# A stage's buffers begin at the weights' address modulo 256, written orders made anew, x loaded first

## The chip, the cores and the metric

The kernel runs on one core of a Trainium2 chip. The metric is the device time of one execution in microseconds (us), the median of several runs. Engines are named as in the profile: PE is TensorE (PEld its weight loads), DVE is VectorE, ACT is ScalarE, POOL is GpSimd, SP is SyncE; an engine's name with a q is its queue, which waits and issues DMAs.

## The reference

A bidirectional encoder of two layers on `x` of 256 tokens by 1024 features, everything in float32. Each layer has three residual parts, so there are six stages:

```
x <- LN(alpha*x + 0.5*SwiGLU_1(x))
x <- LN(alpha*x + Mixer(x))        # layer 0: bidirectional chunkwise mLSTM, layer 1: windowed attention
x <- LN(alpha*x + 0.5*SwiGLU_2(x))
swiglu(x, w_in, w_out) = (silu(x @ w_in[:, :2816]) * (x @ w_in[:, 2816:])) @ w_out
```

The four SwiGLU parts (1024 by 5632 and 2816 by 1024 weights each) are most of the work. The mixers are a projection, a chunk of small per-head work, and an output projection.

## The kernel before

**Float32 products in three passes.** A float32 operand is split into two parts of the type fp32r, a high part (ACT copies and rounds it) and a low part (DVE subtracts the high part from the original). `mm3` (lines 598 to 601) then issues three matmuls: high by high, high by low, low by high. The stationary operand, which a weight load brings into the array before each matmul, is 128 columns of activations. The moving operand, which streams past it, is 512 columns of weights.

**Weights.** `Weights.load` issues a DMA of 512 KB from HBM into a raw buffer of one of two kinds: four `w_raw` tiles that live for the whole kernel, and in the SwiGLU stages eight more, `s_raw`, that belong to the stage. `Weights.split` (lines 382 to 404) lets ACT write one of ten `w_hi` tiles and DVE one of ten `w_lo` tiles from it. The SwiGLU stages compute most of the up projection with seven block products instead of eight (`seven`, line 835; `product`, line 822), for which DVE adds raw weight blocks in place and POOL issues DMAs that add a block from HBM onto a raw buffer.

**Stationary operands.** `xT_hi` and `xT_lo` hold the transposed activations and live for the whole kernel. A stage owns `S1` to `S4` (sums of blocks of the transposed activations, for the seven products), `h` and `hc` (the transposed result of SiLU times up, for the down projection), in the attention stage `q`, `kp` and others, and temporaries `t`.

**Where buffers lie.** Whole-kernel tiles come from ordinary pools. Stage buffers share one region of `4 * WHOLE` bytes per partition at the upper end of SBUF; each stage lays its own buffers out in it from the bottom (`Stage.new`, lines 342 to 353), every buffer size rounded up to 32 bytes, in the order in which the code asks for them. Worked out from the sizes in the code, the start addresses are:

| buffers | start address modulo 256 before |
|---|---|
| `w_raw`, `w_hi`, `w_lo`, `x`, `xT_hi`, `xT_lo`, `neg_id` | 96 |
| `ident` | 128 |
| SwiGLU stages: `h`, `s_raw`, `t`, `S1` to `S4`, `hc` | 64 |
| mLSTM stage: `v` (four tiles) | 64, 96, 128, 160 |
| mLSTM stage: `q`, `k`, gate rows, `wt`, `a`, `ln_g`, `ln_b` | 224 |
| attention stage: `kp`, `sc`, `dist`, `v`, `q` | 224 |
| attention stage: `ln_g`, `ln_b`, `pr0`, `pr1`, `o` | 96 |

**The order of the work.** Code that calls an engine only records the call (`Engine`, line 304). `Program.issue` (line 292) then issues all calls in the order written down in `ORDER` (steps between call numbers), and `Rooms.take` gives each request the buffer that the lists in `SLOTS` name. So the order on every engine's queue and the choice of each buffer in a ring are written lists, made beforehand by a planner that is not part of the kernel. All issued calls carry line 301 in the profile; operations are told apart by the tiles that they write and read.

**The start.** `load_x` (line 558) loads `x` in four parts of 128 tokens by 512 features on ACT's queue. PE transposes a part, ACT and DVE split the result into `xT`, and the first products follow. PE also runs two lots of ten transposes of `ident` to bridge the time until `x` lands.

Of the kernel before, what the change touches and what calls it, by code (L numbers as in the profile page):

```python
# [37 lines left out]
WHOLE = 21800  # L38
ORDER = (
# [210 lines left out]
    "mv": ("010101010101"),  # L250
    "rs": ("010101010101"),
    "raw.1": ("30230230230123012301230123012301"),
    "wt.1": ("0123"),
    "a_hir.1": ("0101"),
    "a_lor.1": ("1010"),
    "den.1": ("0101"),
# [77 lines left out]
class Stage:  # L334
# [7 lines left out]
    def new(self, name, n, bufs, dt):  # L342
        tag = name
# [1100 lines left out]
```

## Time and profile before

| | |
|---|---|
| median of 3 runs | 942.94 us (942.77 to 944.59) |
| the profiled execution's own time | 939.63 us |
| its span, first to last instruction | 937.9 us |
| PE busy | 921.9 us (98% of the span) |
| DVE busy | 814.0 us (87%) |
| ACT busy | 578.4 us (62%) |
| POOL busy | 142.3 us (15%) |
| granted TensorE clock | 0.998 |

A row of instruction groups shows the line, the engine, the operation, what it writes and reads, the shapes and the count; behind the first bar the busy time of the group and the mean duration of one in ns; behind the second the engine's idle time just before, and what ended it. A row of the timeline shows start and duration in us. Matmuls overlap: the next starts before the previous has ended, so the step from start to start is what counts, and it is shorter than the duration shown.

### The profile page before, as it was taken

The numbers are of one execution on the slowest core, as the hardware profiler recorded it, in microseconds if no ns is written. First come the engines' busy times: TensorE is split into PE (matmuls) and PEld (weight loads), VectorE is DVE, ScalarE is ACT, GpSimd is POOL, SyncE is SP. The second block draws the span as 40 slices with busy tenths as digits, with TensorE's granted clock in tenths as the row PEclk, the third lists the DMA queues.
The fourth block names the chain that finished last, engine by engine and source line by source line (L and its number), as shares of the span: only waits on it lengthen the run. The fifth ranks groups of instructions, "written<-read, shape, count | busy, mean of one in ns | idle before, by whom it ended". The sixth has DMA issues, their size and how long they took to land.

```text
span 937.9 us, 12265 instructions
## 1 busy us (share of the span) xinstructions
PE 921.9 (98%) x4368; PEld 757.3 (81%) x4368; DVE 814.0 (87%) x955; ACT 578.4 (62%) x813; POOL 142.3 (15%) x202
## 2 busy tenths in 40 slices
PE   8999999999999999999999999999999999999996
PEld 7887888889988888888888888888887688878885
DVE  6998888886798999889899978898978899987985
ACT  6765577556654667566548575665578567665560
POOL 0411201100100111111011102111444211211110
PEclk9999999999999999999999999999999999999999
DMA  9999898557346699889967997885740487998841
GB/s 345 285 284 275 237 284 211 192 180 226 135 174 254 175 276 233 260 247 244 313 212 200 270 281 183 268 240 181 256 132 4 154 250 228 248 292 230 264 126 45
DMA packets 100637, 208.50 MB, mean 222 GB/s; under 512 B 6848, under 2 KB 21200, under 8 KB 100576
## 3 DMA queue, kind: packets, MB, share of 16 engines
q1 hardware_dynamic: 82368, 173.04, 52.3%
q0 software_dynamic: 17632, 33.64, 21.4%
q10 hardware_dynamic: 576, 1.05, 0.3%
q8 instruction: 34, 0.56, 0.2%
q14 instruction: 27, 0.22, 0.1%
HBM read 206.65 MB, written 1.05 MB: 221 GB/s over the span
## 4 chain that ended last, share of the span: by engine, by line
PE 93%; DMA 2%; DVE 2%; ACT 2%; POOL 0%; issue 0%; POOLq 0%; ACTq 0%
PE p L301 93%; DMA x<-in_x_dram 1%; DMA s_raw<-in_ffn_w_in_dram 1%; DVE pr_lor L301 0%; ACT w_hi L301 0%; ACT sc L301 0%; DVE rm L301 0%; DVE x L301 0%; DVE o L301 0%; POOL sc L301 0%; DVE nm L301 0%; ACT q_hir L301 0%; ACT o L301 0%; DVE w_lo L301 0%; POOL sm L301 0%
## 5 line engine op out<-in xcount | busy, mean ns | idle before, releaser
L301 ACT CAST w_hi<-s_raw 128x1024 fp32r<-128x1024 f32 x237 | 242.4, 1049 | 116.4 <-PE p L301 68.0
L301 DVE TENSOR_TENSOR w_lo<-s_raw,w_hi 128x1024 fp32r<-128x1024 f32 x237 | 282.6, 1218 | 25.3 <-ACT w_hi L301 24.3
L301 ACT CAST w_hi<-w_raw 128x1024 fp32r<-128x1024 f32 (+1 forms) x168 | 174.3, 1046 | 85.2 <-PE p L301 43.3
L301 DVE TENSOR_TENSOR w_lo<-w_raw,w_hi 128x1024 fp32r<-128x1024 f32 (+1 forms) x168 | 202.4, 1218 | 27.6 <-ACT w_hi L301 27.3
L301 PE MATMUL p<-w_hi,xT_hi 128*128 128x512 f32 x512 | 203.7, 398 | 0.0
L301 PE MATMUL p<-w_hi,xT_lo 128*128 128x512 f32 x512 | 200.1, 391 | 0.0
L301 PE MATMUL p<-w_lo,xT_hi 128*128 128x512 f32 x512 | 199.7, 390 | 0.3 <-DVE w_lo L301 0.3
L301 PE MATMUL p<-w_hi,h_hir 128*128 128x512 f32 x320 | 127.3, 398 | 0.0
L301 PE MATMUL p<-w_lo,h_hir 128*128 128x512 f32 x320 | 126.4, 395 | 0.0
L301 PE MATMUL p<-w_hi,h_lor 128*128 128x512 f32 x320 | 126.2, 395 | 0.0
L301 PEld LDWEIGHTS p<-w_hi,xT_lo 128*128 128x128 f32 x512 | 96.1, 188 | 20.4
L301 PEld LDWEIGHTS p<-w_lo,xT_hi 128*128 128x128 f32 x512 | 96.4, 188 | 19.3 <-DVE w_lo L301 0.7
L301 PEld LDWEIGHTS p<-w_hi,xT_hi 128*128 128x128 f32 x512 | 96.4, 188 | 18.4
L301 POOL DMA_DIRECT2D s_raw<-in_ffn_w_in_dram x44 | 53.2, 1210 | 341.6 <-DVE s_raw L301 94.2
L301 PE MATMUL p<-w_hi,S_hir 128*128 128x512 f32 x256 | 101.3, 396 | 0.4 <-ACT t L301 0.4
L301 PE MATMUL p<-w_lo,S_hir 128*128 128x512 f32 x256 | 101.2, 395 | 0.0
L301 PE MATMUL p<-w_hi,S_lor 128*128 128x512 f32 x256 | 101.1, 395 | 0.0
L301 PEld LDWEIGHTS p<-w_hi,h_lor 128*128 128x128 f32 x320 | 60.0, 187 | 14.6
L301 PEld LDWEIGHTS p<-w_lo,h_hir 128*128 128x128 f32 x320 | 60.0, 188 | 14.2
L301 PEld LDWEIGHTS p<-w_hi,h_hir 128*128 128x128 f32 x320 | 60.0, 188 | 14.0
L301 PEld LDWEIGHTS p<-w_hi,S_hir 128*128 128x128 f32 x256 | 48.0, 187 | 12.8 <-ACT t L301 1.1
L301 PEld LDWEIGHTS p<-w_lo,S_hir 128*128 128x128 f32 x256 | 48.0, 187 | 12.1 <-DVE w_lo L301 0.4
(201 smaller groups left out, 1195.4 us busy)
## 6 DMA issues: line engine op xcount, KB each, us to landing
s_raw<-in_ffn_w_in_dram SPq DMA_DIRECT2D x104, 512.0 KB, 6.5
w_raw<-in_ffn_w_in_dram SPq DMA_DIRECT2D x56, 512.0 KB, 6.3
s_raw<-in_ffn_w_out_dram SPq DMA_DIRECT2D x55, 512.0 KB, 6.8
s_raw<-in_ffn_w_in_dram POOLq DMA_DIRECT2D x44, 512.0 KB, 6.4
w_raw<-in_ffn_w_out_dram SPq DMA_DIRECT2D x33, 512.0 KB, 6.6
w_raw<-in_ml_w_in_dram SPq DMA_DIRECT2D x24, 512.0 KB, 4.4
w_raw<-in_ffn_w_in_dram POOLq DMA_DIRECT2D x20, 512.0 KB, 7.8
w_raw<-in_at_w_in_dram SPq DMA_DIRECT2D x12, 512.0 KB, 4.2
```

Source lines behind the costliest of these rows:

```text
L301: f(*args, **kw)
```

## The change

Three things change together.

1. `Stage.new` lays out buffers in two directions. Sizes that are multiples of 64 elements (256 bytes) go up from the bottom, the others come down from the end of the region. `WHOLE` falls from 21800 to 21792 elements, so the region begins 32 bytes later: at 96 modulo 256 in place of 64. As a result `h`, `s_raw`, `t`, `S1` to `S4`, `hc`, `q`, `k`, `kp`, `sc`, `dist`, the attention's `v` and all other buffers of whole 256 bytes begin at 96 modulo 256, as the weights do. The small statistics tiles and the mLSTM's `v` tiles (whose rows are 1032 elements long) lie at the end.
2. `ORDER` and most lists of `SLOTS` are written anew. PE's matmuls keep their order, all 4,368 of them; the order on DVE, ACT, POOL and SP differs in many places, and so do the buffers that are taken from the rings.
3. At the start ACT's queue issues all four parts of `x` one behind the other, the first halves of both token blocks ahead of the second halves, and only then loads its table of functions. Before, one part was issued, then the table was loaded, then two parts were issued, and the fourth after ACT's first evacuation. In the new order a copy stands ahead of the recorded table load, so a table load of its own comes ahead of that copy: ACT has one table load more, 7 in place of 6.

```
-WHOLE = 21800
+WHOLE = 21792
 ORDER = (
-    "0 5 35 -34 63 -65 4 1 75 -74 1 109 -108 1 87 -99 13 1 123 -135 13 1 136 21 -156 1 1 1 3 1 -3 4 1 -25 189 "
...
+    "0 1 1 1 2 35 -34 63 -61 1 75 -74 1 89 -88 1 1 1 1 1 1 156 -155 1 1 22 -19 1 -3 4 1 93 -92 13 -18 6 1 -26 27 "
...
 class Stage:
 
     def __init__(self, rooms, bass_, start, key, kinds):
-        self.rooms, self.bass, self.start, self.key, self.top, self.tags = rooms, bass_, start, key, 0, {}
+        self.rooms, self.bass, self.start, self.key, self.top, self.end, self.tags = rooms, bass_, start, key, 0, WHOLE, {}
...
     def new(self, name, n, bufs, dt):
         tag = name
         if tag not in self.tags:
-            self.tags[tag] = self.top, -(-n // 8) * 8
-            self.top += bufs * self.tags[tag][1]
-            assert self.top <= WHOLE, (tag, self.top)
+            size = -(-n // 8) * 8
+            if size % 64 == 0:
+                self.tags[tag] = self.top, size
+                self.top += bufs * size
+            else:
+                self.end -= bufs * size
+                self.tags[tag] = self.end, size
+            assert self.top <= self.end, (tag, self.top, self.end)
         at, step = self.tags[tag]
```

More of the change, by code (lines that the diff above doesn't have):

```diff
@@ L35 @@
 PEND = [6, 4, 6, 6, 6]
-WHOLE = 21800
+WHOLE = 21792
 ORDER = (
[190 rows of a table removed]
[190 rows of a table added]
 )
 SLOTS = {
-    "p": ("0123456702374502145673565365735653567657360521734652017436452071356201735602614735017524360143751237"
-        "4652140704340347043404373470364523145627136050646046506460645465042671503467021354702615340762453127"
-        "046653644534665364354365436127301267503642461641624616461216"),
+    "p": ("0123456702354702147653767367537673765675360721534672015436472051376201537602614537015724360143571235"
+        "4672140504340345043404353450364723147625136070646046706460647467042651703465021374502615760325674310"
+        "562274266746227426476427642310453120754261623263216232623132"),
     "h_hir.0": ("01010"),
@@ L237 @@
     "raw.0": ("012345678192ab034567a2b30514687905182465317908a24b7198025a46183b0256"),
-    "w_hi": ("0123456789012359071346803259714354307568252914307685291430768529143076852940713685472901368547290136"
-        "8547290136854729013685472901368547290681354729806135428137659041628375904162837590416283759041623598"
-        "7041386259704138625970413869725041387692504372519086429375108642937510864293751086429350871642589307"
-        "1642589307164258930716425893071642589713064258197306451302768943751026894375102689437510268943750681"
-        "294308756129"),
+    "w_hi": ("0123456789012359071346891250734154197568252034197685203419768520341976852049731685472093168547209316"
+        "8547209316854720931685472093168547209683154720896315428317650943628175094362817509436281750943621508"
+        "7943186250794318625079431860725943187602594172530986420175398642017539864201753986420159873642570198"
+        "3642570198364257019836425701983642570831964257308196453192867041853926704185392670418539267041859673"
+        "204197856320"),
     "w_lo": ("0123456789012345678901236457890137826945065137829406513782940651378294065172938406795123840679512384"
         "0679512384067951238406795123840679512384067951328406791285304672391850467239185046723918504672398041"
-        "5672813904567281390456728139045672819304567213089546739210854673921085467392108546739205418673049251"
-        "8673049251867304925186730492518673049251867304295186734950281679234508167923450816792345081679235814"
-        "067951238406"),
+        "5672813904567281390456728139045672819304567213089546739210854673921085467392108546739205418673019254"
+        "8673019254867301925486730192548673019254867301295486731950284679231508467923150846792315084679235841"
+        "067954238106"),
     "t.0": ("03242155040312543102435120431"),
@@ L252 @@
     "raw.1": ("30230230230123012301230123012301"),
-    "wt.1": ("0123"),
+    "wt.1": ("3201"),
     "a_hir.1": ("0101"),
-    "a_lor.1": ("1010"),
+    "a_lor.1": ("0101"),
     "den.1": ("0101"),
@@ L261 @@
     "h_lor.2": ("0101010101"),
-    "raw.2": ("a9b78234061ba9578234ab97526830415260b87a32415690b8421650a9b7263850a79b384501a8749b35012694b531802a67"
-        "318a4059216738ba4061783a9b4518203a95"),
-    "t.2": ("1320154023124503241532045132451043524013025410235104253102"),
-    "sc.4": ("4501230145230145230145"),
-    "raw.4": ("20320320320132013201"),
+    "raw.2": ("a564789236041a5789b214a75968b32059634871b92056a3482906531a4796b85317a4b825301872a4b53096a245b0839167"
+        "b081235a9067b841236078b1a4250893b1a5"),
+    "t.2": ("2354210453250143502135401235012403150423451024531240513245"),
+    "sc.4": ("1405231405231405231405"),
+    "raw.4": ("23123123123012301230"),
     "rm.4": ("01201201"),
@@ L270 @@
     "es.4": ("01201201"),
-    "pr0_hir.4": ("01010101"),
+    "pr0_hir.4": ("10101010"),
     "pr0_lor.4": ("01010101"),
@@ L275 @@
     "o.4": ("01010101"),
-    "h_hir.5": ("10101"),
-    "h_lor.5": ("10101"),
-    "raw.5": ("3201320148596732ab0169723b8a04153b849a260b1538749a1b58346792b80a3462"),
-    "t.5": ("02135043125140321450213405214"),
+    "h_hir.5": ("01010"),
+    "h_lor.5": ("01010"),
+    "raw.5": ("1230123058496712ab3069721b8a35041b859a263b0418759a0b48156792b83a1562"),
+    "t.5": ("51024532014035210345102354103"),
 }
```

378 rows, old and new, of the table ORDER are left out of this document.

## Prediction

> **What bounds the kernel now.** I read the page first, then PE's waits, then the groups of instructions, and last the timeline of PE where it runs without a wait.
>
> ```profile
> span 937.9 us, 12265 instructions
> PE 921.9 (98%) x4368; PEld 757.3 (81%) x4368; DVE 814.0 (87%) x955; ACT 578.4 (62%) x813; POOL 142.3 (15%) x202
> ...
> PE 93%; DMA 2%; DVE 2%; ACT 2%; POOL 0%; issue 0%; POOLq 0%; ACTq 0%
> ```
>
> PE is busy for 98% of the span and is 93% of the chain that ended last. What shortens the stream of matmuls shortens the kernel; what happens beside it does not, unless PE comes to wait for it. So the question is how long one matmul takes, and whether its operands' places in SBUF have a part in that.
>
> ```profile
> L301 PE MATMUL p<-w_hi,xT_lo 128*128 128x512 f32 x512 | 200.1, 391 | 0.0
> L301 PE MATMUL p<-w_lo,xT_hi 128*128 128x512 f32 x512 | 199.7, 390 | 0.3 <-DVE w_lo L301 0.3
> L301 PE MATMUL p<-w_lo,h_hir 128*128 128x512 f32 x320 | 126.4, 395 | 0.0
> L301 PE MATMUL p<-w_lo,S_hir 128*128 128x512 f32 x256 | 101.2, 395 | 0.0
> L301 PE MATMUL p<-w_lo,hc_hir 128*128 128x512 f32 x32 | 12.6, 395 | 0.0
> L301 PE MATMUL p<-w_lo,q_hir 128*128 128x512 f32 x32 | 12.6, 393 | 0.0
> L301 PE MATMUL p<-kp_hir,q_lor 128*128 128x512 f32 x16 | 6.3, 395 | 0.0
> ```
>
> All are the same operation: 512 columns of weights past 128 columns of activations. With `xT` as the stationary operand one takes 390 to 391 ns, with `h`, `S` and `hc` 395. `xT` begins at 96 modulo 256, like the moving `w_hi` and `w_lo`; `h`, `S` and `hc` begin at 64. The mean holds starts after transposes too, so I look at stretches without any, by the step from start to start:
>
> ```profile
> 20.11 0.39 PE L301 MATMUL p<-w_lo,xT_hi 128*128 128x512 f32 x1
> 30.99 0.39 PE L301 MATMUL p<-w_lo,xT_hi 128*128 128x512 f32 x1
> ...
> 73.46 0.39 PE L301 MATMUL p<-w_hi,S_hir 128*128 128x512 f32 x1
> 75.80 0.39 PE L301 MATMUL p<-w_lo,S_hir 128*128 128x512 f32 x1
> ...
> 740.84 0.39 PE L301 MATMUL p<-w_lo,q_hir 128*128 128x512 f32 x1
> 744.32 0.40 PE L301 MATMUL p<-w_lo,q_hir 128*128 128x512 f32 x1
> ...
> 920.07 0.39 PE L301 MATMUL p<-w_lo,h_hir 128*128 128x512 f32 x1
> 929.17 0.39 PE L301 MATMUL p<-w_lo,h_hir 128*128 128x512 f32 x1
> ```
>
> `xT`: 48 steps in 10.88 us, 226.7 ns each. `S`: 10 steps in 2.34 us, 234 ns. `q` (at 224): 15 steps in 3.48 us, 232.0 ns. `h`: 39 steps in 9.10 us, 233.3 ns. Three other reasons for the difference can be looked at in the trace. It isn't the form of the code: `product` issues the same twelve matmuls with `xT` and with `S`. Nor is it traffic on SBUF:
>
> ```profile
> core 0: us, PE busy (x) PEld busy (x) DVE busy (x) ACT busy (x) POOL busy (x), PEclk, DMA share, GB/s
> 20.00:31.00 11.00, 11.00 (x51) 9.09 (x50) 11.00 (x11) 7.76 (x10) 1.24 (x2) 1.00 1.04 396
> 920.00:929.00 9.00, 9.00 (x40) 7.21 (x40) 6.96 (x12) 0.59 (x1) 0.56 (x1) 1.00 0.00 0
> 300.00:350.00 50.00, 50.00 (x229) 40.78 (x228) 48.55 (x54) 31.33 (x39) 6.61 (x6) 1.00 0.81 241
> 750.00:800.00 50.00, 50.00 (x228) 40.93 (x228) 49.41 (x57) 34.17 (x43) 6.32 (x5) 1.00 0.81 246
> ```
>
> The fast stretch has the DMA engines and DVE full; the slow one has no DMA and an idle ACT. And it isn't the clock: 1.00 in both. What is left is where the operands lie.
>
> **The change, part by part.**
>
> *Addresses of stationary operands.* `h`, `S` and `hc` go from 64 to 96, the relation that `xT` has now. Their number from the rows: three of a triple, 3 x (320 + 256 + 32) = 1,824. Per matmul the pure stretches give 233.3 - 226.7 = 6.6 ns, in all 12.0 us; the row means give 395 - 390.5 = 4.5 ns, 8.2 us, because around group starts `xT` is slow as well and will stay so. I take the middle, 5.6 ns: 10.2 us. PE's stream has no cover, so this comes off the end. It supposes that being alike modulo 256, or being at 96, is the cause. The `kp` by `q` row speaks against the first form, since both lie at 224 and take 395; but after the change everything is at 96 beside 96, which is the very case of `xT`.
>
> *The attention's operands.* `q`, `kp` go from 224 to 96: 3 x (32 + 16) = 144 matmuls at 232.0 - 226.7 = 5.3 ns, 0.8 us. In that stage short operations of ACT and DVE set part of the time, so between 0 and 0.8; I take 0.5.
>
> *Raw buffers, temporaries, DMA.* `s_raw` moves from 64 to 96, where `w_raw` already lies:
>
> ```profile
> L301 DVE TENSOR_TENSOR w_lo<-s_raw,w_hi 128x1024 fp32r<-128x1024 f32 x237 | 282.6, 1218 | 25.3 <-ACT w_hi L301 24.3
> L301 DVE TENSOR_TENSOR w_lo<-w_raw,w_hi 128x1024 fp32r<-128x1024 f32 x166 | 201.1, 1224 | 26.9 <-ACT w_hi L301 26.6
> L301 ACT CAST w_hi<-s_raw 128x1024 fp32r<-128x1024 f32 x237 | 242.4, 1049 | 116.4 <-PE p L301 68.0 <-DVE s_raw L301 20.7 <-DMA s_raw<-in_ffn_w_in_dram 11.3
> L301 ACT CAST w_hi<-w_raw 128x1024 fp32r<-128x1024 f32 x166 | 173.1, 1051 | 84.4 <-PE p L301 43.3 <-DMA w_raw<-in_ml_w_in_dram 16.3 <-DMA w_raw<-in_at_w_in_dram 5.4
> ...
> s_raw<-in_ffn_w_in_dram SPq DMA_DIRECT2D x104, 512.0 KB, 6.5
> w_raw<-in_ffn_w_in_dram SPq DMA_DIRECT2D x56, 512.0 KB, 6.3
> ```
>
> DVE and ACT take the same within 6 ns, and the landing differs by 0.2 us with ACT's first reason for waiting being PE. So nothing, on either sign.
>
> *`x` first.* PE waits for the parts of `x`:
>
> ```profile
> PE p L301 <- DMA x<-in_x_dram: 2.0, 2, 1.4
> PE p L301 <- DVE w_lo L301: 0.3, 1, 0.3
> ...
> 1.25 1.28 ACT L301 ACT_TABLE_LOAD   x1 [1.25 <-PEq L1431]
> 5.64 0.59 ACT L301 CAST xT_hi<-p 128x512 fp32r<-128x512 f32 x1 [3.10 <-PE p L301]
> 6.63 0.33 ACTq L301 DMA_DIRECT2D x<-in_x_dram  x1
> 7.00 1.14 ACT L301 CAST w_hi<-w_raw 128x512 fp32r<-128x512 f32 x2 [0.78 <-DMA x<-in_x_dram]
> ...
> 6.63 6.12 DMA x<-in_x_dram
> ...
> 11.05 0.39 PE L301 MATMUL p<-w_hi,xT_lo 128*128 128x512 f32 x1
> 12.79 1.09 PE L301 MATMUL p<-ident,x 128*128 128x128 f32 x8 [1.36 <-DMA x<-in_x_dram]
> ```
>
> The fourth part is issued at 6.63, its wait ends 6.12 us later, and PE, done with its step at 11.05 + 0.23, stands until 12.79: 1.5 us. In the new queue four issues (0.33 us for this one) stand ahead of all of ACT's work, so the last goes out within the first 3 us and with the same 6.12 lands by about 9, before PE asks. What it is moved past on ACT's queue are its first evacuation and the table load; on the DMA engines it now competes with SP's first weights, 256 KB at the 396 GB/s of the first window, 0.65 us, for pieces that PE reads after the first twelve matmuls (2.7 us). Late next are ACT's and DVE's halves of `xT`, which PE reads only after twelve more matmuls. The added table load (1.28 us) lies where ACT idles: 3.10 us before 5.64 and 0.78 before 7.00, into which the first copy of weights moves; with that cover gone it costs up to 1.28. So between 0.2 and 1.8 (with the wait for `w_lo`, 0.3, gone too); I take 1.5.
>
> *The written orders.* PE's order stays. With PE faster, DVE has less room: it is busy for 48.55 and 49.41 of 50 us in the two windows above. Each holds some 110 matmuls that get 5.6 ns shorter, 0.6 us, of which DVE's slack covers 1.45 in the one and 0.59 in the other; I take 0.6 us off in all for such places. What the new orders do otherwise can't be seen in this trace: PE is idle for 937.9 - 921.9 = 16.0 us, of which some 8 lie behind its last matmuls (929.17 and one more); the other 8 are start and waits in between, so new orders can hardly win more than 3 us, and I allow the same for a loss; I take 0.
>
> Sum: 10.2 + 0.5 + 1.5 - 0.6 = 11.6 us. Against the profiled execution's own 939.63 us that is 928.0; that execution is 3.3 us below the median, so for the median 942.94 - 11.6 = 931.3 us.
>
> The Trainium skill, in "TensorE: Matmul & The Clock Gate", Part 2, "Step-by-step: what each phase is for", says that PE has two independent SBUF read ports and that loading the next tile's weights doesn't steal read bandwidth from the running matmul. By that rule the addresses would change nothing and the sum would be 1.5 alone. The steps of 226.7 and 233.3 ns don't fit it; no run here yet moves an operand.
>
> **The rivals.**
>
> *The addresses do nothing.* The difference could go with something else that `h`, `S` and `q` share: all lie in the upper part of SBUF, above `xT`. The `kp` by `q` row speaks for it (equal modulo 256, yet 395). Against it: the `h` tiles follow right on `xT`, at a place that is no round number. Then only `x` first is left: 942.94 - 1.5 = 941.4 us. This is the case of the skill's rule too.
>
> *DVE becomes the bound in the SwiGLU stages.* The windows with 97% and 99% speak for it; its 87% over the span and ACT's waiting for PE speak against it. If half of the 10.2 is lost: 936.4 us.
>
> *Slower: results that PE reads next stand behind one more split on DVE.* In the written orders I count 13 results with less than 1.3 us to spare before that now come after one more DVE operation, mostly a `w_lo`. One of them:
>
> ```profile
> 537.32 0.68 DVE L301 TENSOR_TENSOR h_lor<-p,h_hir 128x512 fp32r<-128x512 f32 x1
> ...
> 538.19 0.39 PE L301 MATMUL p<-w_hi,h_lor 128*128 128x512 f32 x1
> ```
>
> Here 0.19 us are spare. Each such place can cost PE up to 1.22 us, all of them 15.9: 947.2 us. It decides from 10 of the 13 on. Against it: many more results come earlier than before, and an order puts a split ahead where DVE would else idle.
>
> **How the numbers follow.** Forecast 0.72, with its own range 927 to 935 (8.2 or 12.0 for the pairs, `x` and orders as above); addresses do nothing 0.10; DVE takes half 0.11; slower 0.07. The range 926.5 to 940 takes in the first and the third. This kernel tells 0.2% (1.9 us) from no change. Faster: 0.72, 0.11 and 0.02 of the second case, 0.85; within: 0.07; slower: 0.07 and 0.01, 0.08.
>
> **What would show it.** The rows of `h`, `S`, `hc` at 390 to 391 ns and a step near 227; `q` and `kp` alike; `xT` unchanged. No wait of PE for `x` after the first, and the eight transposes at about 11.3. DVE and ACT at 1,218 and 1,049 as before. The prediction is wrong if these rows stay at 395, or if PE's waits grow by more than 3 us.

## The result, and the profile after

The changed kernel takes **930.97 us** (median of 4 runs, 928.99 to 933.04) beside 943.77 us for the kernel before in the same comparison: a ratio of **0.9863, 95% interval 0.9835 to 0.9891**. Run once more in a later comparison it stood at 0.9878 (0.9859 to 0.9897), 929.61 beside 942.06 us. That is 11.5 to 12.9 us by the ratios. One execution of the runs below, of the kernel before with less work for DVE, was slow (2369.51 us) and is left out of every figure. The pair of profiled executions shows less, 939.63 against 931.54 us, because the profiled execution of before was the shortest of that kernel that was seen (its times in four comparisons, three medians and a single execution, lie between 941.5 and 943.8).

The page of the changed kernel, its busy times and its chain by engine:

```profile
span 929.8 us, 12210 instructions
PE 912.3 (98%) x4368; PEld 758.3 (82%) x4368; DVE 809.7 (87%) x955; ACT 578.5 (62%) x814; POOL 148.1 (16%) x202
...
PE 78%; DVE 7%; DMA 5%; issue 4%; ACT 4%; POOL 0%; SPq 0%; POOLq 0%; ACTq 0%; DVEq 0%
```

PE's busy time fell by 9.6 us (921.9 to 912.3), and PE is now 78% of the chain that ended last, no longer 93%: DVE, the DMAs and ACT carry the end in more places. Some of its groups of matmuls (busy time, mean ns of one, idle before and what ended it):

```profile
L301 PE MATMUL p<-w_hi,xT_lo 128*128 128x512 f32 x512 | 200.1, 391 | 0.0
L301 PE MATMUL p<-w_lo,xT_hi 128*128 128x512 f32 x512 | 199.7, 390 | 1.1 <-DVE w_lo L301 1.1
L301 PE MATMUL p<-w_lo,h_hir 128*128 128x512 f32 x320 | 124.7, 390 | 0.8 <-DVE w_lo L301 0.8
L301 PE MATMUL p<-w_lo,S_hir 128*128 128x512 f32 x256 | 99.8, 390 | 0.7 <-DVE w_lo L301 0.7
L301 PE MATMUL p<-w_lo,hc_hir 128*128 128x512 f32 x32 | 12.4, 389 | 0.0
L301 PE MATMUL p<-w_lo,q_hir 128*128 128x512 f32 x32 | 12.5, 391 | 0.0
L301 PE MATMUL p<-kp_hir,q_lor 128*128 128x512 f32 x16 | 6.3, 394 | 0.0
```

The first and the last row of a stretch of its PE timeline without a wait, near the end (start, duration):

```profile
912.22 0.39 PE L301 MATMUL p<-w_lo,h_hir 128*128 128x512 f32 x1
921.31 0.39 PE L301 MATMUL p<-w_hi,h_lor 128*128 128x512 f32 x1
```

`h`, `S` and `hc` went from 395 ns to between 389 and 390, `xT` stayed where it was, and the stretch with `h` makes 40 steps in 9.09 us, 227.3 ns each (233.3 before). Over all 1,813 recorded steps to a matmul with `h`, `S` or `hc` as the stationary operand, those above 245 ns left out as waits, the mean went from 233.3 to 227.1 ns: 11.3 us in all. `kp` by `q` hardly moved.

The two windows in which DVE was full before, in the changed kernel:

```profile
300.00:350.00 50.00, 50.00 (x231) 41.30 (x230) 49.61 (x56) 32.00 (x41) 7.70 (x7) 1.00 0.84 249
750.00:800.00 50.00, 50.00 (x232) 41.51 (x231) 48.59 (x54) 33.53 (x42) 7.82 (x7) 1.00 0.86 250
```

Some of PE's waits in it (us in total, times, longest):

```profile
PE p L301 <- DVE w_lo L301: 2.6, 3, 1.1
PE p L301 <- ACT t L301: 1.1, 2, 0.7
PE p L301 <- DMA x<-in_x_dram: 0.7, 1, 0.7
PE p L301 <- DVE pr_lor L301: 0.5, 1, 0.5
```

DVE now fills 99% of the first window, and PE waits 2.6 us for `w_lo` where it was 0.3. The waits for `x` (2.0 before) and for `pr_lo` have shrunk. For the latter, and for one by POOL that will be needed, the rows of the kernel before:

```profile
PE p L301 <- DVE pr_lor L301: 1.6, 2, 1.2
...
PE p L301 <- POOL sc L301: 0.9, 1, 0.9
```

So four things happened at once: shorter steps, new waits for DVE, fewer waits in the attention stage, an earlier `x`. The experiments take them apart.

### The profile page after: what moved, and what is told of

It is laid out like the page before. It is cut to its first block, busy times and chain, and to the rows that moved or that the text cites. A ratio compares the mean times of both kernels' runs of the same rounds, so it can differ in the third digit from the quotient of the medians.

```text
span 929.8 us, 12210 instructions
## 1 busy us (share of the span) xinstructions
PE 912.3 (98%) x4368; PEld 758.3 (82%) x4368; DVE 809.7 (87%) x955; ACT 578.5 (62%) x814; POOL 148.1 (16%) x202
## 4 chain that ended last, share of the span: by engine, by line
PE 78%; DVE 7%; DMA 5%; issue 4%; ACT 4%; POOL 0%; SPq 0%; POOLq 0%; ACTq 0%; DVEq 0%
PE p L301 78%; DVE w_lo L301 4%; DMA s_raw<-in_ffn_w_in_dram 3%; ACT w_hi L301 2%; DMA w_raw<-in_ffn_w_out_dram 1%; DVE s_raw L301 1%; DMA w_raw<-in_ffn_w_in_dram 1%; DVE t L301 0%; ACT wt L301 0%; DMA x<-in_x_dram 0%; SPq L301 0%; DVE x L301 0%; DVE pr_lor L301 0%; ACT t L301 0%; DVE rm L301 0%
## 5 line engine op out<-in xcount | busy, mean ns | idle before, releaser
L301 DVE TENSOR_TENSOR w_lo<-s_raw,w_hi 128x1024 fp32r<-128x1024 f32 x234 | 278.5, 1218 | 28.7 <-ACT w_hi L301 28.5
L301 DVE TENSOR_TENSOR w_lo<-w_raw,w_hi 128x1024 fp32r<-128x1024 f32 (+1 forms) x171 | 205.2, 1215 | 29.2 <-ACT w_hi L301 28.8
L301 ACT CAST w_hi<-w_raw 128x1024 fp32r<-128x1024 f32 (+1 forms) x171 | 176.9, 1046 | 80.4 <-PE p L301 42.9
L301 POOL DMA_DIRECT2D s_raw<-in_ffn_w_in_dram x42 | 51.1, 1218 | 330.1 <-DVE w_raw L301 87.7
```

The source lines that it names most:

```text
L301: f(*args, **kw)
```

## The experiments

Theory A says that the addresses make the gain; theory B gives it to the new written orders. Three runs with one part each, and one with two parts, in one comparison (the kernel before: 941.53 us).

**The addresses alone.** In the kernel before, `WHOLE` only sets where the region begins (229,344 - 4 x `WHOLE`) and a limit, so one number moves it to another place that is 96 modulo 256, with the order and the layout within the region unchanged:

```diff
-WHOLE = 21800
+WHOLE = 21856
```

> The kernel before, its order and its layout, with one number changed: the region of the stages begins 224 bytes lower, at 96 modulo 256 in place of 64, so that h, S and hc lie at 96 like the weights (q and kp come to lie at 0). Theory A, the addresses make the gain: the rows of h, S and hc go from 395 to 390 or 391 ns, the step from start to start from 233.3 to 227.5 ns, and 1,824 matmuls by 5.8 ns give 10.6 us less, a ratio of 0.989. Theory B, the new orders make it: nothing changes, 0.998 to 1.002.

Measured: 933.39 us, ratio 0.9907 (0.9894 to 0.9921), 8.8 us less by the ratio, 8.1 by the medians. Two groups of this run:

```profile
L301 PE MATMUL p<-w_lo,h_hir 128*128 128x512 f32 x320 | 124.5, 389 | 0.0
L301 PE MATMUL p<-w_lo,S_hir 128*128 128x512 f32 x256 | 99.7, 390 | 0.4 <-DVE w_lo L301 0.4
```

Its chain by engine:

```profile
PE 78%; DVE 8%; DMA 7%; ACT 4%; issue 3%; POOL 1%; POOLq 0%; ACTq 0%; SPq 0%; DVEq 0%
```

Theory B falls: with the old orders the rows are at 389 to 390 ns. But about 2.5 us of the 11.3 that the steps give don't reach the end; the chain hands 15% more to other engines. This is taken up below.

**The changed kernel with its region 32 bytes lower.** It keeps the new orders and the early `x` and gives up the alignment:

```diff
-WHOLE = 21792
+WHOLE = 21800
```

> The changed kernel with its region 32 bytes lower, so that h, S, hc, q and kp begin at 64 modulo 256; its orders and its early x stay. Theory A: the rows of h, S and hc are back at 395 ns and the time at that of the kernel before less what the early x gives (1.0 us): a ratio of 0.999, or 0.996 to 1.002 with the orders unknown. Theory B: still 0.987.

Measured: 937.92 us, ratio 0.9962 (0.9949 to 0.9975). The row of `h` is back at 395 ns. So without the addresses the change is still worth 3.6 us, more than the early `x` gives. Its group of `h`:

```profile
L301 PE MATMUL p<-w_lo,h_hir 128*128 128x512 f32 x320 | 126.5, 395 | 0.3 <-DVE w_lo L301 0.3
```

Two of PE's waits in it show where a part of the 3.6 us is:

```profile
PE p L301 <- DVE pr_lor L301: 0.5, 1, 0.5
...
PE p L301 <- POOL sc L301: 0.2, 1, 0.2
```

In the kernel before these two waits, both of the attention stage, were 1.6 and 0.9 us, as shown above. The wait for `w_lo` grew the other way, from 0.3 to 1.4 us.

**`x` first, alone.** In `ORDER` of the kernel before, calls 1 to 3 move up behind call 0:

```diff
-    "0 5 35 -34 63 -65 4 1 75 -74 1 109 -108 1 87 -99 13 1 123 -135 13 1 136 21 -156 1 1 1 3 1 -3 4 1 -25 189 "
+    "0 1 1 1 2 35 -34 63 -65 4 1 75 -74 1 109 -108 1 87 -86 1 123 -122 1 136 21 -156 1 1 1 3 1 -3 4 1 164 -168 5 "
...
```

> The kernel before with one edit: the four loads of x are issued first on their queue. By the prediction 1.5 us less (0.2 to 1.8); by what the changed kernel's first 13 us show, 1.0 us less, because the eight transposes came 1.0 us earlier there: a ratio of 0.999, at the limit of what the runs can tell. The wait of PE for x before those eight goes.

Measured: 940.76 us, ratio 0.9986 (0.9977 to 0.9995): 0.8 us by the medians, 1.3 (0.5 to 2.2) by the ratio. Its profiled execution doesn't show the gain. PE's timeline there:

```profile
5.46 1.12 PE L301 MATMUL p<-ident,x 128*128 128x128 f32 x4 [1.60 <-DMA x<-in_x_dram]
...
10.21 0.63 PE L301 MATMUL p<-w_hi,xT_lo 128*128 128x512 f32 x1
10.64 0.63 PE L301 MATMUL p<-w_hi,xT_hi 128*128 128x512 f32 x1
11.06 0.51 PE L301 MATMUL p<-w_lo,xT_hi 128*128 128x512 f32 x1
11.41 0.40 PE L301 MATMUL p<-w_hi,xT_lo 128*128 128x512 f32 x1
...
13.01 1.03 PE L301 MATMUL p<-ident,x 128*128 128x128 f32 x8
```

The wait before the eight transposes is gone, but they come at 13.01, not at 11.3, for two reasons: the first part of `x` landed 1 us later than in the profile of before (5.46 against 4.49 us; 4.44 in the run below, which has the same edit), and until 11.06 PE ran at half its pace (a step of 0.43 us in place of 0.23). Further on, near 340 and 827 us, PE waits 2.3 us in all for `t`, where it waited 0.4 in the profile of before. Whether the early `x` brings these waits or they are chance, no run shows.

**Both edits in the kernel before**, the region at 96 and `x` first:

```diff
-WHOLE = 21800
+WHOLE = 21856
...
-    "0 5 35 -34 63 -65 4 1 75 -74 1 109 -108 1 87 -99 13 1 123 -135 13 1 136 21 -156 1 1 1 3 1 -3 4 1 -25 189 "
+    "0 1 1 1 2 35 -34 63 -65 4 1 75 -74 1 109 -108 1 87 -86 1 123 -122 1 136 21 -156 1 1 1 3 1 -3 4 1 164 -168 5 "
...
```

> Both edits in the kernel before, its order otherwise kept: the region at 96 and x first. Theory A and x add: 10.6 and 1.0 us, 0.9877, which would be the whole of the change; then the new orders are worth nothing. If the new orders cost what the changed kernel's new stalls suggest (about 3 us more of steps that are too long than before), this one is faster than the changed kernel, 0.984; if they gained, it is slower than the changed kernel's 0.9863.

Measured: 932.78 us, 0.9907 (0.9891 to 0.9922): 0.6 us less than the addresses alone by the medians, nothing by the ratio. Here too the waits for `t` are longer, 1.8 us against 0.7 with the addresses alone, and take a part of the early start back. The changed kernel's 0.9863 and 0.9878 are below it, with intervals that touch, so the new orders gained rather than lost; of the expectation's readings the one that took their new stalls for a loss falls. PE's start in this run:

```profile
8.19 0.75 PE L301 MATMUL p<-w_hi,xT_hi 128*128 128x512 f32 x1
8.77 0.41 PE L301 MATMUL p<-w_lo,xT_hi 128*128 128x512 f32 x1
...
11.33 1.03 PE L301 MATMUL p<-ident,x 128*128 128x128 f32 x8
```

Two of PE's waits in this run, where those of the attention stage are still as in the kernel before:

```profile
PE p L301 <- DVE pr_lor L301: 1.5, 2, 1.2
PE p L301 <- POOL sc L301: 0.9, 1, 0.9
```

In the timeline PE is at full pace from 8.77 us on, as in the profile of before (from 8.75), and the eight transposes come at 11.33 in place of 12.79: 1.46 us earlier.

**Which property of the addresses counts?** A1: the moving operand of the running matmul and the stationary operand of the next must begin alike modulo 256. A2: the place 96 itself. A3 and A4: a distance of 128 or of 64 does too. Four versions of the changed kernel, each with the time of a single execution; the padding of 128 bytes is one line ahead of the weights (in the third ahead of `xT`), the rest is the number. The first is shown; the second has the padding alone, the fourth only the number, 21840.

```diff
-WHOLE = 21792
+WHOLE = 21824
...
+    state.tile([128, 32], F32, name="pad", tag="pad")
     raws = tiles("w_raw", D, F32, RAW_BUFS)
```

> The changed kernel with 128 bytes of padding ahead of the weights and the region moved with them: weights, xT, h, S, hc, q and kp all begin at 224 modulo 256. Theory A1, what counts is that the running matmul's moving operand and the next one's stationary operand begin alike modulo 256: all steps at 227.5 ns, rows of xT, h, S at 389 to 391 ns, time as the changed kernel's, 931 us. Theory A2, what counts is the place 96 itself: every row at 395, xT's too; 5.8 ns for 1,536 + 1,824 matmuls, 19 us more, 950 us. The kp by q row of the kernel before (both at 224, 395 ns) speaks for A2.

> The same padding, the region left at 96: weights and xT at 224; h, S, hc, q and kp at 96. A1: xT stays at 390 to 391 ns, h, S and hc go back to 395: 1,824 by 5.8 ns, 10.6 us more than the changed kernel, 941 us. A2 for the stationary operand alone: the reverse, xT 395 and h, S, hc 390: 8.9 us more, 940 us. A2 for both operands: all at 395, 950 us.

> The padding behind the weights: weights at 96; xT and the whole region at 224. A1: nothing is alike any more, rows of xT, h, S and hc all at 395, 19 us more than the changed kernel, 950 us. A theory A3, that a distance of 128 will do: as the changed kernel, 931 us. If what counts is only that xT and h are placed alike, also 931 us.

> The changed kernel with the region at 160 modulo 256 (224 to 160 is a move of no other buffer): weights and xT at 96, h, S, hc, q and kp 64 bytes off. A1: h, S and hc at 395 ns, time as that of the region at 64, 938 us. A4, equality modulo 64 is enough: 390 ns and 931 us.

| weights at | `xT` at | `h`, `S`, `hc` at | `xT` by `w_lo` | `h` by `w_lo` | `S` by `w_lo` | time |
|---|---|---|---|---|---|---|
| 224 | 224 | 224 | 390 ns | 390 ns | 390 ns | 934.66 us |
| 224 | 224 | 96 | 391 | 394 | 395 | 936.95 |
| 96 | 224 | 224 | 395 | 395 | 395 | 947.05 |
| 96 | 96 | 160 | 391 | 396 | 395 | 939.66 |

The groups of the first, and below them those of the third, which decide:

```profile
L301 PE MATMUL p<-w_lo,xT_hi 128*128 128x512 f32 x512 | 199.9, 390 | 1.1 <-DVE w_lo L301 1.1
L301 PE MATMUL p<-w_lo,h_hir 128*128 128x512 f32 x320 | 124.8, 390 | 0.2 <-DVE w_lo L301 0.2
```

```profile
L301 PE MATMUL p<-w_lo,xT_hi 128*128 128x512 f32 x512 | 202.0, 395 | 1.0 <-DVE w_lo L301 1.0
L301 PE MATMUL p<-w_lo,h_hir 128*128 128x512 f32 x320 | 126.3, 395 | 0.0
```

A1 holds in all four. With everything at 224 the steps are as short as with everything at 96, so it is no place of its own; with the stationary operands 128 or 64 bytes off, or 32 off as in the run above, they are long, in the third those of `xT` too. A whole 256 bytes make no difference: the region begins 256 bytes lower in the run with the addresses alone (21856) than in the changed kernel (21792), and the rows are the same. That the next matmul's stationary operand counts and not the running one's own is seen where the two kinds meet in the kernel before: 28 steps from a matmul with `xT` to one with `h` have a median of 235 ns, 15 from `h` back to `xT` one of 227.

The times fit less exactly than the rows (931, 941, 950 and 938 us were expected). In the first and the third PE ran at half pace for some 3.5 us in the middle of the kernel (granted clock 0.51 from 682 to 685 us, 0.57 from 250 to 253), an estimated 1.6 us from the steps there; in the second, whose steps are longer, PE waits only 0.3 us for `w_lo`, against 2.0 in the first.

**Does DVE take back what is missing?** From the eleventh piece of weights on, DVE's subtraction covers half the columns, once in the kernel before and once with the region at 96:

```diff
-            nc.vector.tensor_sub(lo, raw, hi.bitcast(F32))
+            n = D if i < RING else 512
+            nc.vector.tensor_sub(lo[:, :n], raw[:, :n], hi[:, :n].bitcast(F32))
```

> The kernel before with less work on DVE: from the eleventh piece of weights on, the subtraction that makes the small part of the weights covers only the first 512 of the 1,024 columns (the other half of the result is left as the buffer had it, so the output isn't the reference's). DVE's 1,218 ns become about 0.65 us, some 220 us less busy time in all. It is the base for the run beside it. If PE's waits of the kernel before are mostly DVE's, it is itself 1 to 3 us faster than the kernel before, 0.997 to 0.999.

> The same with the region at 96 modulo 256, as in the run with the addresses alone. Theory C1: the addresses are worth 1,813 steps by 6.4 ns, 11.6 us, and what of it was missing in the run with the addresses alone (8.1 to 8.8 us in the medians and the ratio) was taken back by waits for DVE; then it is 11 to 12 us faster than the run beside it with the lighter DVE. Theory C2: the steps themselves give only 8 to 9 us at the end, whatever DVE does; then the two are 8 to 9 us apart here too.

Measured: 936.98 and 926.12 us, 0.9948 (0.9935 to 0.9962) and 0.9830 (0.9817 to 0.9844). They are 10.9 us apart by the medians and 11.1 by the ratios, as C1 said. The first alone is 4.9 us faster than the kernel before by the ratio, where 1 to 3 were expected, so DVE's full work cost that kernel more than its waits for `w_lo` show. The chain of the second:

```profile
PE 93%; ACT 2%; DVE 2%; DMA 1%; POOL 0%; issue 0%; POOLq 0%; ACTq 0%
```

One of the two windows in it:

```profile
750.00:800.00 50.00, 50.00 (x234) 41.51 (x233) 36.53 (x53) 34.09 (x42) 7.23 (x6) 1.00 0.92 257
```

With DVE at 73% in that window, PE is back at 93% of the chain and keeps nearly the whole gain of its steps. The same addresses gave 8.1 to 8.8 us with DVE's full work: 2.3 to 2.7 us are lost to it. Each of these ratios is known to some 1.3 us, so this loss is only just clear of the noise.

**The second table load**, and the changed kernel again. In the new order the preload of the table, call 4, comes late; here it stands right behind the loads:

```diff
-    "0 1 1 1 2 35 -34 63 -61 1 75 -74 1 89 -88 1 1 1 1 1 1 156 -155 1 1 22 -19 1 -3 4 1 93 -92 13 -18 6 1 -26 27 "
+    "0 1 1 1 1 1 35 -34 63 -61 1 75 -74 1 89 -88 1 1 1 1 1 1 156 -155 1 1 22 -19 1 -3 4 1 93 -92 13 -18 6 1 1 11 "
...
```

> The changed kernel with the preload of ACT's table (step 37 of its order) moved right behind the four loads of x, so that the table load at 7.09 us (1.28 us) goes. If that load held up the first copies of weights, PE's stretched steps between 8.30 and 9.72 us become regular, the eight transposes come at 11.3 in place of 11.79 and the time is 0.5 us less; if it lay in idle time as predicted, the transposes stay at 11.8 and nothing changes. In the ratio, 0.9858 or 0.9863, which the runs can't tell; the trace decides.

> The changed kernel once more, beside the others and on the same chip: 0.986, and PE's long steps at the places of its first profile (74, 91, 246, 883 and 898 us) if they belong to its order, elsewhere if they are chance.

Measured: 930.18 us (0.9881, 0.9867 to 0.9894) and 929.61 us (0.9878, 0.9859 to 0.9897): no difference. The transposes did come at 11.36, as expected if the load were in the way, but the start shows another reason. PE's start in the changed kernel and, below it, in this run:

```profile
8.30 0.78 PE L301 MATMUL p<-w_hi,xT_hi 128*128 128x512 f32 x1
8.87 0.63 PE L301 MATMUL p<-w_lo,xT_hi 128*128 128x512 f32 x1
9.30 0.59 PE L301 MATMUL p<-w_hi,xT_lo 128*128 128x512 f32 x1
9.72 0.41 PE L301 MATMUL p<-w_hi,xT_hi 128*128 128x512 f32 x1
...
11.79 1.03 PE L301 MATMUL p<-ident,x 128*128 128x128 f32 x8
```

```profile
8.40 0.59 PE L301 MATMUL p<-w_hi,xT_hi 128*128 128x512 f32 x1
8.79 0.59 ACT L301 CAST xT_hi<-p 128x512 fp32r<-128x512 f32 x1 [1.61 <-PE p L301]
8.83 0.39 PE L301 MATMUL p<-w_lo,xT_hi 128*128 128x512 f32 x1
...
11.36 1.04 PE L301 MATMUL p<-ident,x 128*128 128x128 f32 x8
```

ACT's `xT_hi` starts at 8.79 without the second load and at 8.68 with it, so the load didn't hold it up. What differs is the moment at which PE comes to full pace: 8.8 against 9.7 us. The run with both edits, whose only table load lies early as well, and the profile of before had it near 8.8 too, and `x` alone, without that load, at 11.4. So the moment doesn't follow the load, and it is put down to chance. The long steps at 74 and 91 us were there again (0.5 and 1.2 us above a regular one) in the second profile of the changed kernel and belong to its order. The one for `w_lo` near 883 us came again too, 0.3 us above a regular one in place of 1.0; the one for `t` at 898 us did not.

## Why the prediction was right, and where its terms were off

The forecast of 931.3 us and the sum of 11.6 us are within what the runs show (930.97 us; 11.5 to 12.9 us). The direction and the main cause were right; several terms were off by 1 to 2.5 us each and cancelled, so that the sum came out this close is luck. The sign of being wrong, PE's waits longer by more than 3 us, didn't show: PE's idle time went from 16.0 to 17.5 us.

- **Addresses of stationary operands, 10.2 us (8.2 to 12.0).** Right in mechanism, too small: 11.3 us by the steps, 10.9 to 11.1 us at the end where DVE has less to do. The middle between 4.5 and 6.6 ns was the wrong choice: 6.2 ns came. The lower bound came from the rows' means, held up by `xT`'s slow steps after transposes; the pure stretches were the better row.
- **The `kp` by `q` row**, cited against equality modulo 256, was no counter-example. These matmuls come three at a time between others, and after an interruption steps are long also where the operands lie alike: with everything at 96 the row is still 394. `xT`, too, is slow behind transposes: in the kernel before the means of its second to sixth step are 230 to 234 ns, in the changed kernel those of the second to tenth 227 to 233.
- **The attention's operands, 0.5 us (0 to 0.8).** The steps to `q` went from 232.0 to 230.2 ns, 110 of them without the waits, 0.2 us.
- **`x` first, 1.5 us (0.2 to 1.8).** The path was right: transposes at 11.33 (predicted about 11.3) where PE's pace came as early as in the profile of before. The expectation of 1.0 us was read from one profile, in which PE came late to full pace; the interval of the runs (0.5 to 2.2) can't tell it from 1.5. By the runs it is worth 0.8 to 1.3 us alone and 0 to 0.6 on top of the addresses: the first part of `x` and PE's pace vary from execution to execution, and the waits for `t` were longer in both. The added table load cost nothing, as predicted.
- **Places where DVE is full, 0.6 us lost.** The mis-sized term: 2.3 to 2.7 us. The prediction looked at two windows and at how far DVE was from full there; but PE also waits behind single results, in stretches whose average is lower (`w_lo` near 74 and 91 us in the changed kernel, with DVE busy for 91% of 50 to 100 us). The rival in which DVE takes half didn't come, but it pointed to the right place: about a fifth to a quarter went.
- **New orders, 0 (3 either way).** They gained 2.3 us (0.9962 with them and `x`, 0.9986 with `x` alone). The traces put it in the attention stage. From its first transpose of `x` to that of the next stage it takes 93.1 us with the region at 64 and 96.2 with `x` alone; with the region at 96 it takes 92.8 to 93.7 in three profiles of the new orders and 96.2 in the run with both edits. The waits for `pr_lo` and `sc` in it fell by 1.1 and 0.7 us; the rest of its gain is not taken apart. The first stage gives some back, 180.5 to 181.2 us against 178.8 with both edits, with the waits for `w_lo` at 74 and 91 us in it. The trace of before had the waits of the attention stage; the prediction left them out because it couldn't price their new place.
- **The rival of results behind one more split.** One of the 13 places, the `h_lo` near 538 us, did turn into a wait (0.4 us in the groups of the changed kernel), and the waits for `w_lo` grew by 2.3 us. It is there, but small beside 15.9 us.
- **The addresses do nothing** fell with the run of the addresses alone. The rule that stood with it, two independent read ports (the Trainium skill, "TensorE: Matmul & The Clock Gate", Part 2, "Step-by-step: what each phase is for"), can't be the whole of it: the same pair of operands takes 227 or 233 ns by the place of the one relative to the other.

The parts add up: 8.8 (addresses, after DVE's share) + 1.3 (`x`) + 2.3 (orders) = 12.4 us, against 11.5 to 12.9. That they do is in part luck, since the ratio showed nothing of `x` on top of the addresses. Of the kernels that compute the whole, none was faster than the changed one by more than the runs can tell.

## What to carry to other kernels

Where a stream of matmuls with a weight load each bounds the kernel, lay stationary and moving operands at the same address modulo 256: for fp32r and 512 columns it cost nothing here and gave 6.2 ns in 233 for each matmul. Read a row's mean by the steps that make it up, since starts and short groups can hide such a difference or feign one. And before the gain of a faster engine is booked, ask of each result it waits for how long before it was ready: DVE, busy for 87% of the span, took back a fifth to a quarter.

## What the runs showed of the hardware

- The length of a step of 512 columns depends on where the running matmul's moving operand and the next one's stationary operand begin relative to each other modulo 256: 226.7 to 227.1 ns in the mean where alike (at 96 or at 224), 232.4 to 233.3 at 32, 64 and 128 bytes apart. Steps of 256 columns (`xT` past weights) were 119 to 120 ns alike or 128 apart. Why, no run shows; that the loading of the next weights is hampered is only argued.
- After transposes or a start, up to nine steps are longer even where the operands lie alike, by up to 7 ns in the mean.
- At the start PE runs at half pace while the profile's clock column shows 1.00: weight loads of 0.33 us in place of 0.19, steps of 0.43 in place of 0.23. Full pace came between 5.1 and 11.4 us in 14 profiled executions that had much the same start; in the changed kernel's it came 1.0 us later than in the profile of before, and its eight transposes 0.46 us later (11.79) than with both edits in the kernel before (11.33). The Trainium skill, "TensorE: Matmul & The Clock Gate", Part 1, "What's actually happening", tells of a clock that is gated to half until a free-running window of some 3.4 us was busy; the trace agrees in the halving and in the chance of the moment, and the latest came some 6 us after PE's transposes had begun again.
- Later the clock column does show half pace. In three executions PE fell to it for some 3.5 us after waits in a mixer stage: 0.50 from 250 to 252 us in the second profile of the changed kernel, 0.51 and 0.57 in the two runs named with the table, with weight loads of 0.33 us as at the start. The other eleven show no such stretch.
